# Loading v as bf16 with a casting DMA instead of casting it on VectorE and ScalarE

## The chip, the cores and the metric

One core of one Trainium2 chip. The metric is the device time of one execution in microseconds (us); lower is better. The profile's span is about 1.7 us shorter than that time, because it leaves out what lies before the first and after the last instruction. In the profile's lines PE is TensorE (matrix products), DVE is VectorE, ACT ScalarE, POOL GpSimd and SP SyncE; L332 is line 332 of that run's kernel, so one statement has different numbers in different runs.

## The reference

A recurrence over time for each of 16 sequences and 256 channels: a weighted mean of v with running exponential weights built from k, w and u, kept stable by a running maximum. Cut to its core:

```python
# k, v: (16, 2048, 256) float32; w, u: (256,)
for b in range(batch):
    aa = bb = 0; pp = -1e38                       # 256 channels each; shortened
    for t in range(seq_len):
        kk, vv = k[b, t, :], v[b, t, :]
        ww = u + kk
        qq = np.maximum(pp, ww)
        e1 = np.exp(pp - qq)
        e2 = np.exp(ww - qq)
        output[b, t, :] = (e1 * aa + e2 * vv) / (e1 * bb + e2 + 1e-08)
        ww = pp - w + kk
        qq = np.maximum(ww, kk)
        e1 = np.exp(ww - qq)
        e2 = np.exp(kk - qq)
        aa = e1 * aa + e2 * vv
        bb = e1 * bb + e2
        pp = qq
```

## The kernel before

It replaces the recurrence by matrices. Time is cut into chunks of 126 steps, four sequences are one "pair" of tiles (126 x 1024 numbers of k, as many of v; four pairs are one "step" below), and there are 66 pairs (64, and 2 of a short first chunk, the "head"). For each pair: VectorE rounds k (L281), PE multiplies it to exponents X, ScalarE takes one long exponential of X (L313), VectorE multiplies by v (L332), PE forms the sums for the state, the denominator and the numerator, ScalarE inverts the denominator by a logarithm (L517) and an exponential (L522), VectorE multiplies numerator and inverse, and a DMA stores the result. A pair's output follows ten pairs later. The parts that the argument touches, condensed ("..." marks cuts; slices and names are shortened):

```python
AHEAD = 4; HALVES = 8
SHARED = range(2, HALVES)               # pairs whose v ScalarE casts
kpool = tile_pool(bufs=AHEAD); vpool = tile_pool(bufs=AHEAD); vbpool = tile_pool(bufs=2)

def load(n):                            # four pairs ahead
    kr = kpool.tile([128, 4, Dm], F32); vr = vpool.tile([128, 4, Dm], F32)
    ...
        for t, x in ((kr, k), (vr, v)): # k first, then v; SyncE for n < 2, else GpSimd
            K((SP if n < 2 else POOL).dma_start(out=t[0:r, :, :], in_=x[...]))

def round_k(n):
    ...
    K(DVE.tensor_copy(KM[n][0:r, 0:i, :], kr_of.pop(n)[0:r, 0:i, :]))

def cast_v(n):
    vb = vbpool.tile([128, 4, Dm], BF16, tag="vb", name="vb")
    if n in SHARED:
        K(SC.activation(vb[0:r, 0:i, :], vr_of.pop(n)[0:r, 0:i, :], ACT.Copy))
    else:
        K(DVE.tensor_copy(vb[0:r, 0:i, :], vr_of.pop(n)[0:r, 0:i, :]))

def times_v(n):
    K(DVE.tensor_mul(ez[0:r, 1:4:2], ez[0:r, 0:4:2], vb...))

def log_den(n): K(SC.activation(RD[n], DEN[n], ACT.Ln, scale=RS))
def invert(n):  K(SC.activation(RD[n], RD[n], ACT.Exp, scale=-1.0))

matrices_for_sums(); round_k(0); logs(0); cast_v(0)
for n in range(NP + LAG + 2):           # the order on each engine, cut
    load(n + AHEAD); exps(n); round_k(n + 1); num(qp, 0); invert(qi)
    den(q); log_den(q); mult(qp, 0); cast_v(n + 1); logs(n + 1)
    num(qp, 1); times_v(n); sums(n); mult(qp, 1); store(qp)
```

`K` pins each engine's instructions to this order, so an engine that waits for one operand lets nothing later pass.

Of the kernel before, what the change touches and what calls it, by code (L numbers as in the profile page):

```python
# [7 lines left out]
F32 = mybir.dt.float32  # L8
F32R = mybir.dt.float32r
BF16 = mybir.dt.bfloat16  # L10
ALU = mybir.AluOpType
ACT = mybir.ActivationFunctionType
# [10 lines left out]
def kernel(  # L23
# [11 lines left out]
    def K(ins):  # L35

        block, e, new = nc.cur_bb.bb, ins.ins.engine, []
        for i in reversed(block.instructions):
            if i.engine == e:
                new.append(i)  # L40
                if i.name == pinned.get(e):
                    break
        for a, b in zip(new[1:], new):
            tc.add_manual_dep(b, a.name, mybir.DependencyInfo(
                mybir.DependencyClass.NoSync, mybir.DependencyReason.DATA), reason="order")
        pinned[e] = new[0].name
        return ins

    PE, DVE, SC, POOL, SP = nc.tensor, nc.vector, nc.scalar, nc.gpsimd, nc.sync

    B, T, Dm = k.shape
    HS = 63
    TC = 2 * HS
    T0 = T % TC
    NST = T // TC
    D = 2 * Dm
    GB = T0
    NG = 3
    NH = NG * GB
    AHEAD = 4  # L60
    LAG = 10
    HALVES = 8

    SHARED = range(2, HALVES)
    RS = 2.0 ** -43
    LNRS = 43 * 0.6931471805599453
    CAP = 68.0
# [2 lines left out]
    consts = ctx.enter_context(tc.tile_pool(name="consts", bufs=1))  # L70
    kpool = ctx.enter_context(tc.tile_pool(name="kpool", bufs=AHEAD))
    vpool = ctx.enter_context(tc.tile_pool(name="vpool", bufs=AHEAD))
    vbpool = ctx.enter_context(tc.tile_pool(name="vbpool", bufs=2))
    ezpool = ctx.enter_context(tc.tile_pool(name="ezpool", bufs=7))
    rpool = ctx.enter_context(tc.tile_pool(name="rpool", bufs=5))
    small = ctx.enter_context(tc.tile_pool(name="small", bufs=2))
# [13 lines left out]
    pairs = []  # L90
# [6 lines left out]
    kr_of, vr_of = {}, {}  # L97

    def is_head(n):
        return pairs[n][0] < 0  # L100
# [5 lines left out]
    def tiles_of(n):  # L106
        return 1 if pairs[n] == (-1, 1) else 2
# [5 lines left out]

    def load(n):
        kr = kpool.tile([128, 4, Dm], F32, tag="kr", name="kr")
        vr = vpool.tile([128, 4, Dm], F32, tag="vr", name="vr")
        kr_of[n], vr_of[n] = kr, vr
        c, p = pairs[n]
        if is_head(n):
            if p == 1:  # L120
                K(POOL.memset(kr[64:96, 0:2, :], 0.0))
                K(POOL.memset(vr[64:96, 0:2, :], 0.0))
            for t, x in ((kr, k), (vr, v)):
                for g in range(NG):
                    b = 6 * g + 4 * p
                    e = min(b + 2 * tiles_of(n), B)
                    if b < e:
                        K(SP.dma_start(out=t[g * GB:(g + 1) * GB, 0:e - b, :],
                                        in_=x[b:e, 0:T0, :].rearrange("n t d -> t n d")))
        else:  # L130
            t0 = T0 + c * TC
            r = min(128, T - t0)
            for t, x in ((kr, k), (vr, v)):
                K((SP if n < 2 else POOL).dma_start(  # L134
                    out=t[0:r, :, :], in_=x[4 * p:4 * p + 4, t0:t0 + r, :].rearrange("n t d -> t n d")))


    crow = consts.tile([128, Dm], F32, tag="crow", name="crow")
# [7 lines left out]
    for n in range(2):  # L146
        load(n)
# [8 lines left out]
    def select(ap, cmp, fill, base, cm, n, step):  # L156
        K(POOL.affine_select(out=ap, in_=ap, pattern=[[step, n]], compare_op=cmp,
                             fill=fill, base=base, channel_multiplier=cm))
# [21 lines left out]
    K(POOL.memset(cc[:, 5:6], CAP - LNRS))  # L180
    select(cc[:, 4:5], GE, 0.0, -HS, 1, 1, 0)
    select(cc[:, 4:5], GE, 0.0, TC - 1, -1, 1, 0)

    def head_blocks(f):
        fill(f[0:GB, GB:NH], 0.0)
        fill(f[GB:2 * GB, 2 * GB:NH], 0.0)
# [87 lines left out]
    def round_k(n):  # L274
        r = NH if is_head(n) else TC
        i = 2 * tiles_of(n)
        if is_head(n):
            KM[n] = kmh.pop(0)
        else:
            KM[n] = kms[n % 2]  # L280
        K(DVE.tensor_copy(KM[n][0:r, 0:i, :], kr_of.pop(n)[0:r, 0:i, :]))  # L281

    def logs(n):
        kr = NH + 2 if is_head(n) else 128


        if n == HALVES:
            psx[0] = log_banks("psx")
        if n < HALVES:
            X = [psx[0].tile([128, 2, D], F32, tag=f"X{q}", name=f"X{q}") for q in range(2)]  # L290
        else:
            t = psx[0].tile([128, 2, 2, D], F32, tag="X", name="X")
            X = [t[:, 0], t[:, 1], t]
        km = KM.pop(n).rearrange("p (i n) d -> p i (n d)", i=2)
        for q, m in enumerate((NLEh, NLZh) if is_head(n) else (NLE, NLZ)):
            for i in range(tiles_of(n)):
                K(PE.matmul(X[q][:, i, :], m[0:kr, :], km[0:kr, i, :], start=True, stop=True))  # L297
        X_of[n] = X

    def ez_of(n):  # L300
        j = 2 * (n % 2)
        return EZ[n // 2][:, :, j:j + tiles_of(n), :]

    def exps(n):
        if n % 2 == 0:
            EZ[n // 2] = ezpool.tile([128, 4, 4, D], BF16, tag="ez", name="ez")
        i = tiles_of(n)
        X = X_of.pop(n)
        if n < HALVES:
            for q in range(2):  # L310
                K(SC.activation(ez_of(n)[:, 2 * q], X[q][:, 0:i, :], ACT.Exp))  # L311
        else:
            K(SC.activation(ez_of(n)[:, 0:4:2], X[2][:, :, 0:i, :], ACT.Exp))  # L313

    VB = {}

    def cast_v(n):
        r = NH if is_head(n) else TC
        i = 2 * tiles_of(n)
        vb = vbpool.tile([128, 4, Dm], BF16, tag="vb", name="vb")  # L320
        if n in SHARED:
            K(SC.activation(vb[0:r, 0:i, :], vr_of.pop(n)[0:r, 0:i, :], ACT.Copy))  # L322
        else:
            K(DVE.tensor_copy(vb[0:r, 0:i, :], vr_of.pop(n)[0:r, 0:i, :]))  # L324
        VB[n] = vb

    def times_v(n):
        ez = ez_of(n)
        i = tiles_of(n)
        r = NH if is_head(n) else TC  # L330
        vb = VB.pop(n).rearrange("p (i n) d -> p i (n d)", i=2)
        K(DVE.tensor_mul(ez[0:r, 1:4:2], ez[0:r, 0:4:2],  # L332
                         vb[0:r, 0:i, :].unsqueeze(1).broadcast_to([r, 2, i, D])))



# [156 lines left out]
    def widen():  # L493
        first_phase.close()
        for name, bufs in (("den", 1), ("num", 2)):
            wide.append(ctx.enter_context(tc.tile_pool(name="wide" + name, bufs=bufs, space=bass.MemoryType.PSUM)))
# [22 lines left out]
    def invert(n, a=0, b=None):  # L519
        r = rows_of(n)  # L520
        b = tiles_of(n) if b is None else b
        K(SC.activation(RD[n][0:r, a:b, :], RD[n][0:r, a:b, :], ACT.Exp, scale=-1.0))  # L522
# [47 lines left out]
    def small_work(n, where):  # L570
        for f, args in later.pop((n, where), []):
            f(*args)
# [38 lines left out]
    matrices_for_sums()  # L611
    round_k(0)
    logs(0)
    cast_v(0)

    out_at = {n + (LAG - 4 if is_head(n) else LAG): n for n in range(NP)}
    for n in range(NP + LAG + 2):

        q, qi, qp = out_at.get(n), out_at.get(n - 1), out_at.get(n - 2)
        live, more, out_q, out_qi, out_qp = n < NP, n + 1 < NP, q is not None, qi is not None, qp is not None  # L620
        if n == NP:
            widen()
        if n + AHEAD < NP:
            load(n + AHEAD)
        small_work(n, "a3")
        if live:
            exps(n)
        small_work(n, "d0")
        if more:
            round_k(n + 1)  # L630
        small_work(n, "p0")
        if out_qp:
            num(qp, 0)
            if n > NP:
                num(qp, 1)
        small_work(n, "d1")
        small_work(n, "a0")
        small_work(n, "p1")
        if n == NP:
            num(qp, 1)  # L640
        if out_qi and qi < NP - 1:
            invert(qi)
        small_work(n, "a2")
        if out_q:
            if q not in DEN:
                den(q)
            if n == NP + 1:

                den(q + 1)
            if q < NP - 1:  # L650
                log_den(q)
            else:
                for i in range(2):
                    log_den(q, i, i + 1)
                    invert(q, i, i + 1)
        if out_qp:
            mult(qp, 0)
        small_work(n, "d2")
        if more:
            cast_v(n + 1)  # L660
        small_work(n, "d3")
        small_work(n, "a4")
        if more:
            logs(n + 1)
        if live and out_qp:
            num(qp, 1)
        small_work(n, "p3")
        if live:
            times_v(n)
            sums(n)  # L670
        small_work(n, "p2")
        small_work(n, "d4")
        if out_qp:
            mult(qp, 1)
            store(qp)
        small_work(n, "d5")
        small_work(n, "p4")
        small_work(n, "a1")
# [31 lines left out]
```

## Time and profile before

| | before |
|---|---|
| time, median of 3 runs | 321.77 us (321.7 to 326.54) |
| span of the profiled run | 318.9 us |
| start, to the first long exponential L313 | 36.77 us |
| next seven pairs, to the L313 at 63.68 us | 26.91 us |
| regular stage, 50 pairs, to 282.45 us | 218.77 us |
| tail | 36.45 us |

The prediction shows the busy totals, the steps of the regular stage and its groups. In the groups of the same seven regular steps (count, then busy us and mean ns, then idle time before and what ended it), the long exponential, and the rounding of k:

```profile
L313 ACT ACTIVATE ez<-X 128x2048 bf16<-128x2048 f32 x28 | 52.4, 1873 | 3.6 <-PE num L530 3.3
...
L281 DVE CAST km<-kr 126x1024 fp32r<-126x1024 f32 x28 | 19.0, 680 | 0.0
```

The rounding took 680 ns, against 777 for v's cast of the same size. Of v's casts the 14 that overlapped with one DMA issue of GpSimd took 685 ns and the 14 that overlapped with two took 868. And VectorE's timeline in the first 20 us (start, duration, instruction, and in brackets the idle time before it with its releaser):

```profile
7.29 0.69 DVE L324 CAST vb<-vr 126x1024 bf16<-126x1024 f32 x1 [0.49 <-DMA vr<-in_v_dram]
8.87 0.70 DVE L281 CAST km<-kr 126x1024 fp32r<-126x1024 f32 x1 [0.88 <-DMA kr<-in_k_dram]
...
17.82 0.42 DVE L281 CAST kmh<-kr 96x512 fp32r<-96x512 f32 x1 [2.46 <-DMA kr<-in_k_dram]
```

The second rounding of k stands at 8.87 us behind the first cast of v, and at 17.82 us VectorE has stood 2.46 us for a load of k that was queued behind loads of v.

### The profile page before, as it was taken

What the parts mean: (1) busy time and instruction counts of PE and PEld (TensorE: products, weight loads), DVE (VectorE), ACT (ScalarE), POOL (GpSimd) and SP (SyncE); (2) the same over time, 40 slices, a digit from 0 to 9 for tenths busy, and PEclk for the clock granted to TensorE, in tenths of its full rate; (3) what the DMA queues carried; (4) which work ended last, traced back from release to release, by engine and by line L of the source; (5) the groups of instructions that cost most, each with busy time, mean ns of one, the idle gap of its engine ahead of it and who ended that gap; (6) DMA issues with size and microseconds to landing.
All of it is one profiled execution on the core that took longest, in us unless ns stands there. A gap on an engine that the chain in (4) does not pass through costs nothing. (4 is left out here: it accounts for less than half of the span.)

```text
span 318.9 us, 3968 instructions
## 1 busy us (share of the span) xinstructions
PE 277.0 (87%) x1132; PEld 125.3 (39%) x1132; DVE 277.7 (87%) x561; ACT 277.6 (87%) x318; POOL 167.3 (52%) x224
## 2 busy tenths in 40 slices
PE   1787699799999999999999999999999999888960
PEld 1323344344434444444444444444444444333420
DVE  5758879989999999999999999999999999887760
ACT  6679699599898989999898989899998989698990
POOL 7445428656465665465665646565546665112430
PEclk9999999999999999999999999999999999999995
DMA  6999996999999999999999999999999999944885
GB/s 203 277 332 348 349 328 159 337 329 344 353 351 352 347 365 377 375 341 350 375 380 367 366 366 373 363 346 373 373 369 351 347 322 306 290 170 163 286 257 154
DMA packets 34486, 102.97 MB, mean 323 GB/s; under 512 B 6618, under 2 KB 10478, under 8 KB 34464
## 3 DMA queue, kind: packets, MB, share of 16 engines
q0 software_dynamic: 27248, 98.23, 89.8%
q1 hardware_dynamic: 7184, 4.47, 5.4%
q8 instruction: 9, 0.15, 0.2%
q14 instruction: 13, 0.11, 0.1%
q10 hardware_dynamic: 32, 0.02, 0.0%
HBM read 68.12 MB, written 34.05 MB: 320 GB/s over the span
## 5 line engine op out<-in xcount | busy, mean ns | idle before, releaser
L313 ACT ACTIVATE ez<-X 128x2048 bf16<-128x2048 f32 x58 | 108.6, 1873 | 7.6 <-PE num L530 5.2
L558 POOL DMA_DIRECT2D out_dram<-rd x63 | 53.4, 847 | 117.6 <-issue 40.9
L538 DVE TENSOR_TENSOR rd<-num,rd 128x512 f32<-128x512 f32 (+2 forms) x131 | 88.7, 685 | 11.1 <-ACT rd L522 6.2
L332 DVE TENSOR_TENSOR ez<-ez,vb 126x2048 bf16<-126x2048 bf16 (+1 forms) x66 | 79.7, 1207 | 3.7 <-ACT ez L311 3.1
L517 ACT ACTIVATE rd<-den 128x1024 f32<-128x1024 f32 (+3 forms) x67 | 66.9, 998 | 12.2 <-PE den L508 11.6
L522 ACT ACTIVATE rd<-rd 128x1024 f32<-128x1024 f32 (+3 forms) x67 | 69.3, 1035 | 0.3
L297 PE MATMUL X<-km,NLE 128*128 128x512 f32 x128 | 51.8, 486 | 13.9 <-DVE km L281 9.9
L134 POOL DMA_DIRECT2D kr<-in_k_dram x62 | 56.4, 910 | 11.1 <-DVE km L281 3.6
L134 POOL DMA_DIRECT2D vr<-in_v_dram x62 | 49.9, 806 | 7.8 <-ACT vb L322 4.8
L530 PE MATMUL num<-ez,LfN 128*128 128x512 bf16 x128 | 49.2, 384 | 4.1 <-DVE rd L538 0.8
L530 PE MATMUL num<-ez,IdN 126*128 126x512 bf16 (+1 forms) x131 | 49.8, 380 | 0.0
L324 DVE CAST vb<-vr 126x1024 bf16<-126x1024 f32 x60 | 45.6, 760 | 1.2 <-DMA vr<-in_v_dram 1.1
L362 PE MATMUL tot<-ez,OHV 126*48 126x512 bf16 x128 | 38.9, 385 | 7.7 <-DVE ez L332 6.6
L281 DVE CAST km<-kr 126x1024 fp32r<-126x1024 f32 x64 | 44.0, 687 | 1.9 <-DMA kr<-in_k_dram 1.9
L297 PE MATMUL X<-km,NLZ 128*128 128x512 f32 x128 | 40.9, 402 | 0.1
L362 PE MATMUL tot<-ez,OHE 128*48 128x512 bf16 x128 | 40.1, 395 | 0.0
L508 PE MATMUL den<-ez,Id 126*128 126x512 bf16 (+1 forms) x131 | 39.1, 378 | 0.0
L508 PE MATMUL den<-ez,Lf 128*128 128x512 bf16 x128 | 38.0, 377 | 0.8 <-DVE tsum L385 0.4
L297 PEld LDWEIGHTS X<-km,NLE 128*128 128x128 f32 x128 | 23.6, 192 | 26.7 <-DVE km L281 6.9
L297 PEld LDWEIGHTS X<-km,NLZ 128*128 128x128 f32 x128 | 24.4, 192 | 6.5 <-ACT ez L311 1.0
L362 PEld LDWEIGHTS <-OHV 126*48 126x48 bf16 x128 | 13.4, 104 | 29.5 <-issue 20.4
L530 PEld LDWEIGHTS <-LfN 128*128 128x128 bf16 x128 | 12.3, 96 | 28.6 <-issue 25.5
(104 smaller groups left out, 204.6 us busy)
## 6 DMA issues: line engine op xcount, KB each, us to landing
out_dram<-rd POOLq DMA_DIRECT2D x60, 512.0 KB, 7.0
kr<-in_k_dram POOLq DMA_DIRECT2D x58, 512.0 KB, 7.9
vr<-in_v_dram POOLq DMA_DIRECT2D x58, 512.0 KB, 8.5
kr<-in_k_dram POOLq DMA_DIRECT2D x4, 504.0 KB, 10.7
vr<-in_v_dram POOLq DMA_DIRECT2D x4, 504.0 KB, 12.0
kr<-in_k_dram SPq DMA_DIRECT2D x2, 512.0 KB, 5.0
vr<-in_v_dram SPq DMA_DIRECT2D x2, 512.0 KB, 6.1
ez<-row SPq DMA_DIRECT2D x64, 8.0 KB, 6.3
```

What stands on the lines that cost most here:

```text
L134: K((SP if n < 2 else POOL).dma_start(out=t[0:r, :, :], in_=x[4 * p:4 * p + 4, t0:t0 + r, :].rearrange("n t d -> t n d")))
L297: K(PE.matmul(X[q][:, i, :], m[0:kr, :], km[0:kr, i, :], start=True, stop=True))
L313: K(SC.activation(ez_of(n)[:, 0:4:2], X[2][:, :, 0:i, :], ACT.Exp))
L324: K(DVE.tensor_copy(vb[0:r, 0:i, :], vr_of.pop(n)[0:r, 0:i, :]))
L332: K(DVE.tensor_mul(ez[0:r, 1:4:2], ez[0:r, 0:4:2], vb[0:r, 0:i, :].unsqueeze(1).broadcast_to([r, 2, i, D])))
L362: K(PE.matmul(TOT[c], m[0:r, :], ez_of(n)[0:r, q, i, :], start=n == first_of[c] and i == 0 and q == 0, stop=n == last_of[c] and i == tiles ...
L508: K(PE.matmul(d[:, i, :], m[0:r, :], ez_of(n)[0:r, q, i, :], start=q == 0, stop=q == 2, skip_group_check=True))
L517: K(SC.activation(RD[n][0:r, a:b, :], DEN[n][0:r, a:b, :], ACT.Ln, scale=RS))
L522: K(SC.activation(RD[n][0:r, a:b, :], RD[n][0:r, a:b, :], ACT.Exp, scale=-1.0))
L530: K(PE.matmul(d, m[0:r, :], ez_of(n)[0:r, q, i, :], start=q == 1, stop=q == 3, skip_group_check=True))
L538: K(DVE.tensor_mul(RD[n][0:r, i, :], NUM.pop((n, i))[0:r, :], RD[n][0:r, i, :]))
L558: K(eng.dma_start(out=out[4 * p + a:4 * p + b, t0:t0 + r, :].rearrange("n t d -> t n d"), in_=o[0:r, a:b, :]))
```

## The change

v is to arrive as bf16: the DMA casts it, only GpSimd's queue issues it, and no engine casts it. So the 60 casts on VectorE, the 6 on ScalarE and their buffers go; the multiplication reads the loaded tile. The first two loads of v follow GpSimd's setup, so that the start of k is not delayed.

```diff
-        vr = vpool.tile([128, 4, Dm], F32, tag="vr", name="vr")
+        vr = vpool.tile([128, 4, Dm], BF16, tag="vr", name="vr")
 ...                                        # head: k on SyncE, v on GpSimd
-            for t, x in ((kr, k), (vr, v)):
-                K((SP if n < 2 else POOL).dma_start(
-                    out=t[0:r, :, :], in_=x[4 * p:4 * p + 4, t0:t0 + r, :]...))
+            K((SP if n < 2 else POOL).dma_start(
+                out=kr[0:r, :, :], in_=k[4 * p:4 * p + 4, t0:t0 + r, :]...))
+            if n >= 2:
+                load_v(n)                   # POOL.dma_start into vr_of[n]
 ...                                        # after GpSimd's setup of masks:
+    for n in range(2):
+        load_v(n)
 ...
-    def cast_v(n): ...                      # and vbpool, SHARED, both calls
 ...
-        vb = VB.pop(n).rearrange("p (i n) d -> p i (n d)", i=2)
+        vb = vr_of.pop(n)[:, 0:2 * i, :].rearrange("p (i n) d -> p i (n d)", n=2)
```

More of the change, by code (lines that the diff above doesn't have):

```diff
@@ L62 @@
     HALVES = 8
-    SHARED = range(2, HALVES)
     RS = 2.0 ** -43
@@ L72 @@
     vpool = ctx.enter_context(tc.tile_pool(name="vpool", bufs=AHEAD))
-    vbpool = ctx.enter_context(tc.tile_pool(name="vbpool", bufs=2))
     ezpool = ctx.enter_context(tc.tile_pool(name="ezpool", bufs=7))
@@ L122, in load @@
                 K(POOL.memset(vr[64:96, 0:2, :], 0.0))
-            for t, x in ((kr, k), (vr, v)):
+            for t, x, eng in ((kr, k, SP), (vr, v, POOL)):
                 for g in range(NG):
@@ L127, in load @@
                     if b < e:
-                        K(SP.dma_start(out=t[g * GB:(g + 1) * GB, 0:e - b, :],
+                        K(eng.dma_start(out=t[g * GB:(g + 1) * GB, 0:e - b, :],
                                         in_=x[b:e, 0:T0, :].rearrange("n t d -> t n d")))
@@ L132, in load, with load_v @@
             r = min(128, T - t0)
-            for t, x in ((kr, k), (vr, v)):
-                K((SP if n < 2 else POOL).dma_start(
-                    out=t[0:r, :, :], in_=x[4 * p:4 * p + 4, t0:t0 + r, :].rearrange("n t d -> t n d")))
+            K((SP if n < 2 else POOL).dma_start(
+                out=kr[0:r, :, :], in_=k[4 * p:4 * p + 4, t0:t0 + r, :].rearrange("n t d -> t n d")))
+            if n >= 2:
+                load_v(n)
+    def load_v(n):
+        c, p = pairs[n]
+        t0 = T0 + c * TC
+        r = min(128, T - t0)
+        K(POOL.dma_start(out=vr_of[n][0:r, :, :],
+                         in_=v[4 * p:4 * p + 4, t0:t0 + r, :].rearrange("n t d -> t n d")))
     crow = consts.tile([128, Dm], F32, tag="crow", name="crow")
@@ L313, in exps @@
             K(SC.activation(ez_of(n)[:, 0:4:2], X[2][:, :, 0:i, :], ACT.Exp))
-    VB = {}
-    def cast_v(n):
-        r = NH if is_head(n) else TC
-        i = 2 * tiles_of(n)
-        vb = vbpool.tile([128, 4, Dm], BF16, tag="vb", name="vb")
-        if n in SHARED:
-            K(SC.activation(vb[0:r, 0:i, :], vr_of.pop(n)[0:r, 0:i, :], ACT.Copy))
-        else:
-            K(DVE.tensor_copy(vb[0:r, 0:i, :], vr_of.pop(n)[0:r, 0:i, :]))
-        VB[n] = vb
     def times_v(n):
@@ L330, in times_v @@
         r = NH if is_head(n) else TC
-        vb = VB.pop(n).rearrange("p (i n) d -> p i (n d)", i=2)
+        vb = vr_of.pop(n)[:, 0:2 * i, :].rearrange("p (i n) d -> p i (n d)", n=2)
         K(DVE.tensor_mul(ez[0:r, 1:4:2], ez[0:r, 0:4:2],
-                         vb[0:r, 0:i, :].unsqueeze(1).broadcast_to([r, 2, i, D])))
+                         vb[0:r].unsqueeze(1).broadcast_to([r, 2, i, D])))
     TOT, SUMS = {}, {}
@@ L613 @@
     logs(0)
-    cast_v(0)
     out_at = {n + (LAG - 4 if is_head(n) else LAG): n for n in range(NP)}
@@ L658 @@
         small_work(n, "d2")
-        if more:
-            cast_v(n + 1)
         small_work(n, "d3")
```

## The prediction

> **What bounds the kernel now.** I read the page first: busy shares, then the 40 slices.
>
> ```profile
> PE 277.0 (87%) x1132; PEld 125.3 (39%) x1132; DVE 277.7 (87%) x561; ACT 277.6 (87%) x318; POOL 167.3 (52%) x224
> ...
> DVE  5758879989999999999999999999999999887760
> ...
> DMA  6999996999999999999999999999999999944885
> GB/s 203 277 332 348 349 328 159 337 329 344 353 351 352 347 365 377 375 341 350 375 380 367 366 366 373 363 346 373 373 369 351 347 322 306 290 170 163 286 257 154
> ```
>
> Three engines have equal totals, so totals decide nothing. The slices show a start (to about 60 us), a long even middle, and a tail from about 285 us. In the tail nothing is multiplied by v any more (the last casts of v start at 280.3 us), so the change can only act in the first two.
>
> In the timeline of ScalarE the long exponential (L313) repeats with a pattern of four: 119.66, 137.11, 154.46 and so on. One such step is four pairs of tiles. The stretches view over these steps, cut at those starts, gives two neighbouring steps and the mean of seven (us busy by engine, then clock, DMA share, GB/s):
>
> ```profile
> 154.46:171.89 17.43, 16.48 (x70) 7.52 (x70) 16.73 (x33) 16.14 (x19) 10.00 (x13) 1.00 1.03 377
> 171.89:189.22 17.33, 16.39 (x70) 7.53 (x70) 16.63 (x33) 16.15 (x19) 10.35 (x13) 1.00 1.02 365
> ...
> sum 121.81, PE 115.03 PEld 52.70 DVE 116.95 ACT 113.01 POOL 71.47; mean PE 16.43 PEld 7.53 DVE 16.71 ACT 16.14 POOL 10.21
> ```
>
> A step lasts 121.81 / 7 = 17.40 us. VectorE fills 16.71 of it (96%), PE 16.43 (its ends are modelled, so that is too much), ScalarE 16.14. VectorE is the bound, by little. The groups of the same seven steps say what it does and why the other two wait (count, busy us, mean ns, then idle before and its releaser):
>
> ```profile
> L332 DVE TENSOR_TENSOR ez<-ez,vb 126x2048 bf16<-126x2048 bf16 x29 | 35.2, 1213 | 0.0
> L517 ACT ACTIVATE rd<-den 128x1024 f32<-128x1024 f32 x28 | 28.5, 1018 | 5.2 <-PE den L508 5.2
> L134 POOL DMA_DIRECT2D vr<-in_v_dram x28 | 22.3, 795 | 0.0
> L324 DVE CAST vb<-vr 126x1024 bf16<-126x1024 f32 x28 | 21.8, 777 | 0.0
> L362 PE MATMUL tot<-ez,OHV 126*48 126x512 bf16 x56 | 16.6, 377 | 3.0 <-DVE ez L332 2.4
> L475 PE MATMUL den<-It,ab 128*128 128x128 bf16 x7 | 1.6, 229 | 2.0 <-DVE ab L469 2.0
> ```
>
> ScalarE idles 5.2 us at L517 and 3.6 us at L313, 8.8 in 7 steps: 1.26 us of each step, all of its gap (17.40 - 16.14), always released by PE. PE in turn idles 3.0 + 2.0 us for VectorE's results. So ScalarE's gap is VectorE's lateness passed on through PE.
>
> **What the Trainium skill says.** (1) "VectorE: DVE Perf Modes", section "Mode 2×_2P": a single-source fp32 copy with both ends in SBUF yields two results per cycle; with that page's 0.96 GHz and some 150 cycles of overhead, (1024 / 2 + 150) / 0.96 = 690 ns. The trace agrees: the casts of v have a median of 687 ns. (2) "SBUF — State Buffer", section "Who interferes with whom": such a cast takes the port pair shared with GpSimd for the whole instruction, and GpSimd's descriptor writing and the cast block each other. The trace agrees in kind: the casts range from 679 to 997 ns and GpSimd's issues from 748 to 1306. Removing the casts removes both. (3) "DMA: Bandwidth & Descriptors", section "SWDGE vs HWDGE vs iDMA": a cast in a DMA must be issued by GpSimd. That fits the change, which moves v's first loads off SyncE; this trace has no casting DMA. (4) The same page, section "Where 436 GB/s comes from": the 16 engines share a ceiling of 435 GB/s. The trace reaches 366 over these steps, 377 in its best step and 380 in its best slice. No page that I found gives the rate of a casting DMA; that is the large unknown here.
>
> **The change part by part.** The order of instructions on each engine was compared: VectorE 540 to 480 rows (60 casts gone), ScalarE 320 to 314 (6 casts gone), PE unchanged at 1755, GpSimd 209 to 213, SyncE 14 to 9. No other compute instruction moves relative to its neighbours.
>
> VectorE in the middle: four casts a step, 21.8 / 7 = 3.1 us. It falls from 16.7 to 13.6 us a step. The multiplication L332 reads bf16 in the same shape as before, so it should stay at 1213 ns. VectorE then stops being the bound, and what is left is ScalarE at 16.14 us a step, untouched there (its six casts of v are all before 32.2 us).
>
> ScalarE's limit: of its 1.26 us idle per step I leave 0.3, since the dependence of L517 on PE remains. Step 16.45 us, 0.95 saved. The regular stage runs from the L313 at 63.68 to the one at 282.45: 51 pairs, 12.75 steps. 12.75 x 0.95 = 12.1 us.
>
> DMA's limit: a step moves 366 GB/s x 17.40 us = 6.37 MB (1.57 MB for each pair's k, v and output, and small rows). If a casting load costs what a plain one does, the best step's 377 GB/s gives 16.9 us and the best slice's 380 gives 16.8. Then only 0.5 to 0.6 us a step can be had: some 7 us.
>
> Start: ScalarE spends 5.9 us on six casts (mean 989 ns) between 14 and 32 us, where it is 85% busy (17.08 of 20 us in the stretch 20 to 40). I count half, 3 us, and give 1 back because v's first seven transfers now follow GpSimd's setup and go through one queue. Net 2 us.
>
> GpSimd: 10.21 us of 17.40 busy. Its v issue would have to grow from 0.80 to over 2.6 us (7.2 us of slack over four) before it binds. Hidden.
>
> Buffers: v's slot is now released by L332 rather than by the cast, nearly a pair later. It is needed again by the L332 four pairs on, 17 us, and v lands in 8.6 us (at most 9.6 between 100 and 200 us). Hidden too.
>
> Sum: 321.8 - 12.1 - 2 = 307.7 if ScalarE sets the pace, 321.8 - 7 - 2 = 312.8 if the DMA engines do. I take 310.
>
> **The rivals.**
>
> *The DMA engines become the bound at plain cost.* For it:
>
> ```profile
> out_dram<-rd POOLq DMA_DIRECT2D x60, 512.0 KB, 7.0
> kr<-in_k_dram POOLq DMA_DIRECT2D x58, 512.0 KB, 7.9
> vr<-in_v_dram POOLq DMA_DIRECT2D x58, 512.0 KB, 8.5
> ```
>
> These are DMA issues with their size and the median us to landing. A pair's three transfers at 377 GB/s need 4.2 us together, but each takes 7 to 8.5: the queue is already deep. Against it: VectorE waits for a load only 1 us in all for v and 1.9 + 2.5 for k. The output tiles are recycled after five pairs; a store issued at the end of the third and landing 7 us later leaves L517 about 2.5 us of slack, so this is where saturation would show first. Result 312 to 316.
>
> *The casting DMA is slower than a plain one*, per byte or because its bf16 runs are half as long (now 98.23 MB in 27,248 packets, 3.6 KB each). Then DMA sets the step outright: at 1.5 times the cost for v a step is 6.37 x 3.5 / 3 / 0.377 = 19.7 us, the whole about 349; at twice, 22.5 us and 385. Nothing in the profile speaks against it. That the writer kept the other two transfers plain and placed v's loads with care is weak evidence that it pays.
>
> *The casting DMA is cheaper*, since it writes half the bytes: a step could then move in 6.37 x 2.5 / 3 / 0.377 = 14.1 us. ScalarE binds, giving 305 to 309.
>
> *PE is the next bound instead of ScalarE.* In the tail, matmuls of 512 columns start 0.22 us apart; 64 of them a step are 14.1 us, and I estimate 15 with the small ones. Below ScalarE, so at most it keeps 0.5 us more of the idle time: 313 or so.
>
> **Range and chances.** I give cheaper or equal casting 75% (305 to 316, nearly all of it more than 2% faster, that is under 315.3), slower casting 20% (over 328), and 5% to a loss elsewhere that cancels the gain. Range 302 to 336: the floor is ScalarE with no gaps at all in the middle (1.26 x 12.75 = 16 us) and 4 us at the start; the top takes in a casting load some 20% dearer. Faster 0.66, within 2% 0.15, slower 0.19.
>
> **What would show it right or wrong.** Right: VectorE's total near 277.7 - 45.6 = 232 us, ScalarE's near 272, the pattern of L313 at 16.3 to 16.9 us a step with ScalarE over 96% busy, and PE's waits for VectorE nearly gone. DMA as bound: new idle time at L517 released by the output's DMA, or at the casts of k and at the multiplication released by a load, with landing times over 9 us. Wrong: v's landing at 12 us or more, a step longer than 17.4 us, GB/s lower at an unchanged DMA share, or many more packets of under 2 KB.

## The result, and the profile after

Before's runs are the three of above and a fourth.

| | runs | median | lowest to highest |
|---|---|---|---|
| before | 4 | 323.56 us | 321.70 to 326.54 |
| after | 4 | 300.01 us | 299.37 to 302.48 |

The ratio is 0.9306, 95% interval 0.9223 to 0.9389. Here and below a ratio is the mean time of one kernel's fast runs over that of the other's in the same rounds, so it is not quite the ratio of the medians quoted. The outcome, with a correct result, is faster by 6.9%; it lies below the forecast range of 302 to 336.

The page of after (busy totals, VectorE's slices, the granted TensorE clock in 40 slices of 7.5 us, and the queue that carries k, v and the output: packets, MB, share):

```profile
PE 271.8 (90%) x1132; PEld 124.5 (41%) x1132; DVE 248.3 (83%) x501; ACT 270.3 (90%) x312; POOL 160.7 (53%) x231
...
DVE  4777768967998989999998999898989898878660
...
PEclk9995999999999999999999999999999999999996
...
q0 software_dynamic: 52896, 82.78, 101.6%
```

VectorE fell below PE and ScalarE. The packets nearly doubled (27,248 to 52,896); the share is the time that packets took, and it passes 100% where they overlap. The "5" in the clock row, at 23 to 30 us, makes this profiled run the slowest of the four (302.48 us): its start is disturbed. The start of e3 below, which only adds copies that turn out harmless and had no such dip, serves as the undisturbed one:

| stage | before | after (this run) | e3 (no dip) |
|---|---|---|---|
| to the first long exponential | 36.77 | 35.06 | 32.90 |
| next seven pairs | 26.91 | 25.39 | 25.50 |
| regular stage, 50 pairs | 218.77 | 203.80 | 202.52 |
| tail | 36.45 | 36.55 | 35.58 |
| span | 318.9 | 300.8 | 296.5 |

In the stretches view each row of after is eight pairs, so two of the steps of before (length, then us busy by engine, clock, DMA share, GB/s):

```profile
146.18:178.34 32.16, 32.02 (x139) 14.93 (x139) 29.51 (x57) 31.80 (x37) 18.71 (x24) 1.00 1.17 330
178.34:210.48 32.14, 32.02 (x139) 14.90 (x139) 29.50 (x57) 31.79 (x36) 18.72 (x24) 1.00 1.17 329
...
sum 128.57, PE 128.04 PEld 59.55 DVE 118.04 ACT 127.19 POOL 75.16; mean PE 32.01 PEld 14.89 DVE 29.51 ACT 31.80 POOL 18.79
```

A step is 128.57 / 8 = 16.07 us, where it was 17.40. ScalarE fills 31.80 of 32.14 (98.9%), PE 32.01 by its modelled ends, VectorE 29.51 (92%). The groups of these four rows:

```profile
L322 ACT ACTIVATE ez<-X 128x2048 bf16<-128x2048 f32 x33 | 62.0, 1879 | 1.7 <-PE num L527 1.5
...
L329 DVE TENSOR_TENSOR ez<-ez,vr 126x2048 bf16<-126x2048 bf16 x33 | 40.2, 1217 | 0.0
...
L514 ACT ACTIVATE rd<-den 128x1024 f32<-128x1024 f32 x32 | 32.7, 1021 | 0.0
...
L290 DVE CAST km<-kr 126x1024 fp32r<-126x1024 f32 x32 | 26.5, 828 | 0.0
...
L359 PE MATMUL tot<-ez,OHV 126*48 126x512 bf16 x64 | 19.1, 379 | 0.0
...
L472 PE MATMUL den<-It,ab 128*128 128x128 bf16 x8 | 1.8, 229 | 0.1
```

L514 is L517 of before: its idle time, 5.2 us in seven steps, is gone altogether; 1.7 us in eight steps remain at the long exponential (L313, now L322; 3.6 in seven before). PE's waits for VectorE, 3.0 and 2.0 us before, are down to 0.0 and 0.1 (L359, L472). The multiplication by v is as fast as before (1217 against 1213 ns). The rounding of k (L281, now L290) grew from 680 to 828 ns. The DMA issues of after (size, median us to landing):

```profile
out_dram<-rd POOLq DMA_DIRECT2D x60, 512.0 KB, 7.5
kr<-in_k_dram POOLq DMA_DIRECT2D x58, 512.0 KB, 8.1
vr<-in_v_dram POOLq DMA_DIRECT2D x60, 256.0 KB, 7.2
```

v lands sooner than before (7.2 against 8.5 us), k and the output a little later (8.1 against 7.9, 7.5 against 7.0).

### The profile page after: what moved, and what is told of

The parts are those of the page before. It is cut to its first block, busy times and chain, and to the rows that moved or that the text cites. A ratio compares the mean times of both kernels' runs of the same rounds, so it can differ in the third digit from the quotient of the medians.

```text
span 300.8 us, 3949 instructions
## 1 busy us (share of the span) xinstructions
PE 271.8 (90%) x1132; PEld 124.5 (41%) x1132; DVE 248.3 (83%) x501; ACT 270.3 (90%) x312; POOL 160.7 (53%) x231
## 2 busy tenths in 40 slices
DMA packets 58485, 85.94 MB, mean 286 GB/s; under 512 B 6834, under 2 KB 42406, under 8 KB 58464
## 3 DMA queue, kind: packets, MB, share of 16 engines
q0 software_dynamic: 52896, 82.78, 101.6%
HBM read 68.12 MB, written 34.05 MB: 340 GB/s over the span
## 5 line engine op out<-in xcount | busy, mean ns | idle before, releaser
L322 ACT ACTIVATE ez<-X 128x2048 bf16<-128x2048 f32 x58 | 108.9, 1877 | 3.3 <-PE num L527 1.8
L329 DVE TENSOR_TENSOR ez<-ez,vr 126x2048 bf16<-126x2048 bf16 (+1 forms) x66 | 79.8, 1209 | 4.1 <-ACT ez L320 2.0
L555 POOL DMA_DIRECT2D out_dram<-rd x63 | 52.6, 835 | 48.0 <-issue 17.9
L514 ACT ACTIVATE rd<-den 128x1024 f32<-128x1024 f32 (+3 forms) x67 | 67.0, 1000 | 4.4 <-PE den L505 3.4
L290 DVE CAST km<-kr 126x1024 fp32r<-126x1024 f32 x64 | 51.2, 801 | 3.0 <-DMA kr<-in_k_dram 3.0
L130 POOL DMA_DIRECT2D kr<-in_k_dram x62 | 47.4, 764 | 0.2 <-issue 0.2
L359 PE MATMUL tot<-ez,OHE 128*48 128x512 bf16 x128 | 40.5, 399 | 0.0
L359 PE MATMUL tot<-ez,OHV 126*48 126x512 bf16 x128 | 39.1, 387 | 1.0 <-DVE ez L329 0.9
L359 PEld LDWEIGHTS <-OHV 126*48 126x48 bf16 x128 | 13.6, 106 | 17.6 <-issue 4.9
L505 PEld LDWEIGHTS <-Lf 128*128 128x128 bf16 x128 | 12.4, 98 | 19.9 <-issue 6.6
```

The source lines that it names most:

```text
L322: K(SC.activation(ez_of(n)[:, 0:4:2], X[2][:, :, 0:i, :], ACT.Exp))
L329: K(DVE.tensor_mul(ez[0:r, 1:4:2], ez[0:r, 0:4:2], vb[0:r].unsqueeze(1).broadcast_to([r, 2, i, D])))
L359: K(PE.matmul(TOT[c], m[0:r, :], ez_of(n)[0:r, q, i, :], start=n == first_of[c] and i == 0 and q == 0, stop=n == last_of[c] and i == tiles ...
L505: K(PE.matmul(d[:, i, :], m[0:r, :], ez_of(n)[0:r, q, i, :], start=q == 0, stop=q == 2, skip_group_check=True))
L514: K(SC.activation(RD[n][0:r, a:b, :], DEN[n][0:r, a:b, :], ACT.Ln, scale=RS))
L555: K(eng.dma_start(out=out[4 * p + a:4 * p + b, t0:t0 + r, :].rearrange("n t d -> t n d"), in_=o[0:r, a:b, :]))
```

## The experiments

The theory: VectorE's casts were the bound, and taking them away is the whole gain. The rivals: the lighter DMA traffic is the gain or the new limit; the load order or ScalarE's six casts are. Results are medians with lowest and highest; each set ran on one chip, beside runs of the kernel before (medians 320.95 to 323.51 us over the sets). One run each of e1 and e3, and three of before's (327.03 to 328.83 us), counted as slow and are not in the ratios. e6 and e7 have two runs each and their verdict is "unclear"; what is read from them is the step.

**e1, v stays a plain f32 load and nothing casts it.** Its output is wrong, which doesn't matter for the time. The multiplication reads a constant; a one-column copy keeps the wait for v.

```diff
-        vr = vpool.tile([128, 4, Dm], BF16, ...)
+        vr = vpool.tile([128, 4, Dm], F32, ...)
-        vb = vr_of.pop(n)[:, 0:2 * i, :].rearrange(...)
+        K(DVE.tensor_copy(touch[0:r, :], vr_of.pop(n)[0:r, 0, 0:1]))
+        vb = ones[:, 0:2 * i, :].rearrange(...)     # constant bf16 tile
```

> The changed kernel, but v is loaded as plain fp32 (512 KB each, same queue and order) and the multiplication reads a constant bf16 tile; a one-column read of v's tile on VectorE, ahead of the multiplication, keeps the wait for the load and frees its slot. Wrong result on purpose (v is replaced by 1). No engine and no DMA casts v. Theory A (all of the gain is the casts' time on VectorE and ScalarE; the DMA's own cost does not matter): about 300 us, a step of 16.1 us as in the changed kernel. Theory B (DMA relief: at plain cost the 16 engines cap the step at the 377 to 380 GB/s taken for the prediction, so the smaller transfer is needed for the last part of the gain): step 16.8 us, 308 to 312 us, with new idle time at the logarithm of the denominators released by the stores, or at the casts of k.

Measured: 299.97 us (297.34 to 303.17), ratio 0.9276 (0.918 to 0.9371). Two neighbouring steps in the stretches view:

```profile
158.79:190.96 32.17, 31.83 (x137) 14.96 (x139) 29.07 (x65) 31.82 (x37) 18.72 (x25) 1.00 1.03 397
```

The same step as after, at 397 GB/s instead of 329. (The count takes a casting load at its bf16 size; read from HBM are 68.12 MB in before, after and e1 alike.) So the lighter traffic is not needed for the gain, and 377 to 380 GB/s, which I had taken for the DMA engines' limit, was only what the kernel before asked for.

**e2, after with spare casts back on VectorE.** They sit where v's casts were and read rounded k, which is already there: only VectorE's time comes back, without a wait for v.

```diff
+    def spare_cast(n):                    # called where cast_v was
+        if n not in range(2, HALVES):
+            vb = vbpool.tile([128, 4, Dm], BF16, tag="vb", name="vb")
+            K(DVE.tensor_copy(vb[0:r, 0:i, :], KM[n][0:r, 0:i, :].bitcast(F32)))
```

> The changed kernel, with spare casts of the same shape (126x1024 fp32 to bf16, from k's rounded tile into a tile that nobody reads) put back on VectorE at the places of the old ones, for all pairs whose v VectorE used to cast (60). v still comes by casting DMA. Correct result. Theory A: the regular stage goes back to about 17.4 us a step, and the whole to about 317 to 319 (the start keeps its gain). Theory B: a good part of the gain stays, step under 16.9 us, under 312 us.

Measured: 323.28 us (322.08 to 323.79), ratio 1.0013 (0.9926 to 1.0101). All of the gain is gone, with v still arriving as bf16. The step is 17.85 us, longer than before's 17.40, and the time is past the 317 to 319 of theory A. The groups of eight regular steps show why:

```profile
L331 DVE CAST vb<-km 126x1024 bf16<-126x1024 f32 x32 | 27.8, 868 | 0.0
L291 DVE CAST km<-kr 126x1024 fp32r<-126x1024 f32 x32 | 26.3, 822 | 0.0
```

Both kinds of cast are now slowed; e8 takes that up.

**e3, after with the six spare casts back on ScalarE.**

```diff
+        if n in range(2, HALVES):
+            K(SC.activation(vb[0:r, 0:i, :], KM[n][0:r, 0:i, :].bitcast(F32), ACT.Copy))
```

> The changed kernel, with only the six early casts put back on ScalarE (spare ones, same shape and places, from k's rounded tile, read by nobody). Correct result. If the gain of 3.2 us in the start is the six casts that ScalarE no longer makes, 302.5 to 303.5 us; if the start is set by loads or by the chain of k's cast and PE, under 301.

Measured: 298.73 us (298.1 to 303.45), ratio 0.9258 (0.9178 to 0.9338), no slower than after. ScalarE's six casts cost nothing at the start; the 3 us that I counted for them had been no gain.

**e4, after with the copy of the sums moved from ScalarE to VectorE** (0.59 us on ScalarE in each step, out of PSUM, where PE's results lie in this program), to see whether ScalarE binds.

```diff
-        K(SC.activation(ts, TOT.pop(c), ACT.Copy))
+        K(DVE.tensor_copy(ts, TOT.pop(c)))
```

> The changed kernel, with the copy of the sums out of PSUM (48x512, 0.59 us, one a step, 17 in all) moved from ScalarE to VectorE, which has 1.3 us of slack a step. Correct result. If ScalarE sets the step now (15.9 of 16.07 us busy): 0.4 to 0.5 us a step less, 293 to 296 us. If PE does (16.0 of 16.07 us by the modelled ends): 299 to 301, and ScalarE's idle time grows by what was taken off.

Measured: 300.29 us (300.04 to 303.3), ratio 0.9334 (0.9253 to 0.9416), step 16.20 us. No gain, and ScalarE is no longer full: 124.58 of 129.62 us (96%), with new idle time in its groups:

```profile
L322 ACT ACTIVATE ez<-X 128x2048 bf16<-128x2048 f32 x32 | 60.4, 1887 | 2.7 <-PE num L527 2.7
...
L514 ACT ACTIVATE rd<-den 128x1024 f32<-128x1024 f32 x32 | 32.9, 1027 | 2.3 <-PE den L505 2.3
```

By the expectation this is the case in which PE sets the step. But the trial was not clean: it puts the copy on VectorE ahead of the multiplication, on which PE waits. So it neither confirms nor refutes ScalarE as the bound.

**m1 to m4, the transfers by themselves.** Their outputs are wrong, which doesn't matter for the times. Only DMAs, one queue, four slots per input: 64 loads of k, 64 of v, 64 stores in m1 and m2; v alone in m3 and m4. Between the two of a pair only v's tile differs:

```diff
-        vr = vpool.tile([128, 4, Dm], F32, ...)     # m1, m3
+        vr = vpool.tile([128, 4, Dm], BF16, ...)    # m2, m4
```

> DMA traffic alone: the 64 loads of k (512 KB), 64 of v (512 KB, plain fp32) and 64 stores (512 KB) in turn from one GpSimd queue with four slots per input, no computing (wrong result on purpose: ones are stored). This is the DMA floor of the kernel before. Theory B: 16.6 to 17.0 us per four pairs (377 to 380 GB/s), so over 265 us; theory A: clearly under 16 us per four pairs, under 255 us.

> The same traffic with v cast to bf16 by the DMA. If a casting load costs what a plain one does: within 2% of the plain traffic. If its cost follows the bytes written (one sixth of all written bytes less): up to 16% less. If casting is slower per byte: longer than the plain traffic, but under 16 us per four pairs, since the changed kernel runs at 16.07.

> Only the 64 plain loads of v, four slots: 33.5 MB at some 350 to 400 GB/s, 85 to 96 us plus the start.

> Only the 64 casting loads of v: the same time if reads set the pace, half of it if writes do, longer if the cast is slow.

Measured: m1 268.1 us (266.87, 269.34), m2 256.55 us (256.42, 256.68); m3 105.45 and m4 102.88 us, one run each. The queue's row in m1:

```profile
q0 software_dynamic: 27648, 100.68, 100.2%
```

and in m2:

```profile
q0 software_dynamic: 52224, 83.90, 114.7%
```

A casting load of v costs about what a plain one does per byte read (span 101.1 against 103.7 us for v alone), and the mixed traffic takes 4.3% less by the medians (4.8% in the spans, 254.7 against 267.6) although the packets nearly double. Four pairs' plain traffic needs 267.6 / 16 = 16.7 us here, as theory B had it. But that is more than the step that e1 reached with the same loads (16.08): this trial, with four slots (buffers) behind one queue, does not measure the engines' ceiling either.

**e5, before with after's load order only.** v stays plain and cast.

```diff
-            for t, x in ((kr, k), (vr, v)):      # head: SyncE for both
+            for t, x, eng in ((kr, k, SP), (vr, v, POOL)):
 ...                                              # load_v split out of load
+    for n in range(2):                           # after GpSimd's setup
+        load_v(n)
```

> The kernel before (all casts on engines, plain loads), with only the order of the first loads taken from the change: v's first seven transfers leave the SyncE queue and are issued by GpSimd at the places where the change issues them. Correct result. If the start's gain (first ScalarE instruction of L313 at 32.6 to 32.9 us in undisturbed runs of the changed kernel and of its variants, against 36.8) is k's transfers no longer queued behind v's: that instruction at 33 to 34 us, and 318 to 319.5 us in all. If it is the removed casts' waits for v's landing: unchanged, 321 to 323.

Measured: 322.41 us (321.65 to 322.97), ratio 1.0011 (0.9938 to 1.0085). The order alone gains nothing: the first long exponential starts at 38.23 us, later than before's 36.77, because VectorE stands 4.52 us at its first cast for a v that now comes later. With this order the start gains only where VectorE no longer waits for v there (after, against e5 and e12).

**e6, e4 together with e7's relief of PE; e7, PE relieved alone.** Their outputs are wrong, which doesn't matter for the times. One of four matmuls of a pair's sums is left out.

```diff
-            for i in range(tiles_of(n)):                      # e6 and e7
+            for i in range(1 if q == 1 else tiles_of(n)):
-                            stop=n == last_of[c] and i == tiles_of(n) - 1 and q == 1,
+                            stop=n == last_of[c] and i == 0 and q == 1,
-        K(SC.activation(ts, TOT.pop(c), ACT.Copy))            # e6 only
+        K(DVE.tensor_copy(ts, TOT.pop(c)))
```

> The changed kernel with PE and ScalarE both relieved: the second of the two matmuls that sum the v half is left out for each pair (0.22 us of PE per pair, 0.87 us a step; wrong result on purpose), and the copy of the sums is on VectorE as in the run before. If PE sets the changed kernel's step of 16.07 us and ScalarE is next: a step of 15.4 to 15.6 us. If the DMA engines do: still 15.9 to 16.1.

> The changed kernel with PE alone relieved in the same way (wrong result on purpose). If PE sets the step and ScalarE is next, at 15.9 us: 15.85 to 15.95 us a step. If ScalarE and PE bind each other only through their waits: 15.7 or less. If the DMA engines bind: 16.0 to 16.1.

Measured: e6 300.57 us (299.95, 301.19), ratio 0.9335 (0.9225 to 0.9444), step 16.21. e7 298.43 us (298.43, 298.44), ratio 0.9268 (0.9163 to 0.9374), step 16.03. Six steps of e7:

```profile
95.06:191.26 96.20, 91.78 (x391) 42.66 (x391) 87.93 (x169) 95.41 (x109) 56.18 (x72) 1.00 1.17 329
```

With PE down to 95% busy the step hardly moves, and ScalarE stays at 99.2%: PE does not bind. (The expectation had a step of 16.0 to 16.1 under "the DMA engines bind", which e1's 397 GB/s rules out; it had no case in which ScalarE alone binds. e6's step fits none of its cases.) That e6 keeps e4's step says that e4's loss was not PE's lack of time. In e6's timeline one pair of the four is shorter and the next longer (4.66 us); I put that down to the chain from the multiplication through the sums, their copy and the one shared PSUM bank to the next logarithm. No run isolates that chain, so this stays an argument.

**e8, e2 with five slots for v.**

```diff
-    vpool = ctx.enter_context(tc.tile_pool(name="vpool", bufs=AHEAD))
+    vpool = ctx.enter_context(tc.tile_pool(name="vpool", bufs=AHEAD + 1))
```

> The changed kernel with the 60 spare casts on VectorE, as before, and five slots for v instead of four, so that v's load no longer waits for the multiplication to free its slot. Correct result. The run with four slots took 17.85 us a step against 17.40 in the kernel before, with the casts of k at 822 ns instead of 680. If this excess is GpSimd writing v's descriptors just when VectorE's casts want the shared ports: the casts fall back to about 700 to 750 ns and the step to 17.4 to 17.5 us, 316 to 318 us in all. If it comes from elsewhere: unchanged, 322 to 324.

Measured: 318.86 us (318.13 to 319.6), ratio 0.9911 (0.9823 to 0.9998), step 17.45 us. The groups:

```profile
L331 DVE CAST vb<-km 126x1024 bf16<-126x1024 f32 x32 | 25.4, 794 | 0.0
L291 DVE CAST km<-kr 126x1024 fp32r<-126x1024 f32 x32 | 21.8, 680 | 0.0
```

k's rounding is back at 680 ns. In after v's slot comes free only with the multiplication, so GpSimd issues v's load later, and it falls on the rounding of k: the 24 of 32 roundings that overlapped with an issue of v took 877 ns, the other 8 took 682. A fifth slot removes that wait and the overlap. With it, VectorE's time in the middle equals before's and so does the step (17.45 against 17.40): the whole gain of the regular stage is VectorE's time. What is left of the gain, 0.9% (its interval barely leaves out 1), lies at the start, whose first long exponential comes at 33.75 us.

**e9, e3 with the real v as source**, so that ScalarE also waits for v, as before.

```diff
+            K(SC.activation(vb[0:r, 0:i, :], vr_of[n][0:r, 0:i, :], ACT.Copy))   # n in 2..7
```

> The changed kernel with the six early casts back on ScalarE as in the earlier run that cost nothing, but now reading v's own tile, so that they wait for v's landing as the old casts did (bf16 to bf16, same shape, nobody reads the result). If the start's gain is the casts' early wait for v: the first ScalarE exponential over four banks moves from 32.9 us to 34.5 or later, and the whole to 300.5 to 303. If not: 298 to 300, as with the spare casts that read k.

Measured: 299.64 us (298.56 to 301.02), ratio 0.9279 (0.9227 to 0.9331), first long exponential at 32.95 us. ScalarE's casts cost nothing at the start, with their wait or without.

**e10, after with half of each inversion left out**: a relief of ScalarE that gives no other engine more to do. Its output is wrong, which doesn't matter for the time.

```diff
-        K(SC.activation(RD[n][0:r, a:b, :], RD[n][0:r, a:b, :], ACT.Exp, scale=-1.0))
+        K(SC.activation(RD[n][0:r, a:a + 1, :], RD[n][0:r, a:a + 1, :], ACT.Exp, scale=-1.0))
```

> The changed kernel with ScalarE alone relieved, and nothing added on VectorE: the exponential that inverts the denominators runs over half of its columns (0.43 us less per pair, 1.7 us a step; wrong result on purpose). If ScalarE's amount of work sets the step of 16.07 us: 15.5 us or less, the rest being PE or a chain of waits, some 290 us in all. If PE or the DMA engines set it: 16.0 to 16.1 us and 299 to 300.

Measured: 296.56 us (295.02, 298.09), ratio 0.9181 (0.9094 to 0.9268). Eight steps:

```profile
94.61:221.45 126.84, 126.78 (x553) 59.12 (x553) 117.69 (x224) 115.60 (x144) 75.09 (x97) 1.00 1.18 333
```

The step falls to 126.84 / 8 = 15.86 us, by 0.21, though ScalarE got 1.45 us a step less to do ((127.19 - 115.60) / 8). That is neither of the two cases expected. PE's share by its modelled ends says little here, as it was at 99.6% in after too. But ScalarE's idle time, 11.2 us in these eight steps, is now all released by PE, and no two neighbouring starts of matmuls lie more than 0.45 us apart (in before about four a step do). So ScalarE binds after, and PE comes next, 1.3% behind.

**e11, after with five slots for v** (the edit of e8 on after).

```diff
-    vpool = ctx.enter_context(tc.tile_pool(name="vpool", bufs=AHEAD))
+    vpool = ctx.enter_context(tc.tile_pool(name="vpool", bufs=AHEAD + 1))
```

> The changed kernel with five slots for v instead of four, otherwise the same. Correct result. The casts of k should go from 828 ns back to about 680 ns in the even middle. If VectorE is off the path that sets the step: no change, 16.0 to 16.1 us a step, 299 to 301 us in all; if its lateness still shows through: 0.1 to 0.3 us a step, 296 to 298.

Measured: 299.15 us (298.38 to 302.44), ratio 0.9289 (0.9211 to 0.9368), step 16.06 us. k's rounding is back at 684 ns in the even middle, and the time does not change: VectorE is off the path, so the collision with GpSimd is harmless in after. No version that I ran is clearly faster than after and correct.

**e12, after with a VectorE copy of v for the first two pairs only.** This gives back the in-order wait for v at the start and nothing else.

```diff
+        if n < 2:
+            K(DVE.tensor_copy(vb[0:r, 0:i, :], vr_of[n][0:r, 0:i, :]))
```

> The changed kernel with only the first two casts of v back on VectorE at their old places, reading v's own tile (spare: bf16 to bf16, read by nobody), so that VectorE, which works in order, waits for v's landing before it casts the second tile of k and before it builds the head's matrices. The run with only the loads' order changed stood 4.5 us at the first of these. If this wait is what costs the start its gain: the first ScalarE exponential over four banks moves from 32.6 to 33.4 us to 35 to 38 us, and the whole to 302 to 304. If not: no change, and the start's gain stays unexplained.

Measured: 302.92 us (302.62 to 303.14), ratio 0.9379 (0.9324 to 0.9434), first long exponential at 37.32 us. VectorE's timeline in e12:

```profile
11.10 0.43 DVE L330 COPY vb<-vr 126x1024 bf16<-126x1024 bf16 x1 [4.53 <-DMA vr<-in_v_dram]
11.44 0.69 DVE L291 CAST km<-kr 126x1024 fp32r<-126x1024 f32 x1
```

and in after:

```profile
7.62 0.69 DVE L290 CAST km<-kr 126x1024 fp32r<-126x1024 f32 x1 [1.10 <-DMA kr<-in_k_dram]
...
14.07 0.42 DVE L290 CAST kmh<-kr 96x512 fp32r<-96x512 f32 x1
```

Two copies of 0.43 us cost some 3 to 4 us (302.92 against 299.15 to 300.01). They do it by the 4.53 us for which VectorE stands, with the second rounding of k behind it (11.44 instead of 7.62 us): from the first long exponential on, e12 is as fast as e3 (263.9 against 263.6 us to the end).

## Why the prediction was wrong

The mechanism held; the sizes did not. VectorE was the bound, its casts were the reason, and ScalarE sets the pace now. But 14 us of gain were summed where about 22 came (6.94% of some 323), and 2.3 of those 14 were then taken off again for a DMA limit at a rate that e1 exceeds. Three terms failed: ScalarE's step of 16.45 us, the limit of the DMA engines, and the 2 us of the start. Between the two undisturbed profiles, before and e3, the spans differ by 22.4 us: 5.3 in the first two stages, 16.3 in the regular one, 0.8 in the tail.

- **VectorE is the bound, its lateness reaches ScalarE through PE: right.** L517's idle time is gone, PE's waits for VectorE are gone, and e2 and e8 give the regular stage's whole gain back with VectorE's time alone.
- **ScalarE's limit, 16.45 us a step and 12.1 us in the regular stage: mis-sized.** The step is 16.07 us; the stage shrank by 15.0 us (after) to 16.3 us (e3). (It has 50 pairs, 12.5 steps, not 51 and 12.75: 12.1 should have been 11.9.) Two terms were off. First, I left 0.3 us of idle time per step; the rows of after leave 32.14 - 31.80 = 0.34 in two steps, 0.17 in one. Second, I took ScalarE's 16.14 us of records as its floor; at full load the same work shows as 15.90. The timeline shows how. In before, with waits between:

```profile
153.08 1.03 ACT L517 ACTIVATE rd<-den 128x1024 f32<-128x1024 f32 x1 [0.74 <-PE den L508]
154.46 1.88 ACT L313 ACTIVATE ez<-X 128x2048 bf16<-128x2048 f32 x1 [0.35 <-PE num L530]
```

In after, without:

```profile
149.22 1.01 ACT L514 ACTIVATE rd<-den 128x1024 f32<-128x1024 f32 x1
150.12 1.88 ACT L322 ACTIVATE ez<-X 128x2048 bf16<-128x2048 f32 x1
151.88 0.26 ACT L448 ACTIVATE y<-AB 128x64 f32<-128x64 f32 x1
```

Back to back, an instruction starts before the record of the one ahead ends: 150.12 is 0.90 us after 149.22, whose record lasts 1.01; 151.88 is 1.76 after 150.12, recorded at 1.88. Each wait that vanishes takes about 0.1 us of recorded busy time with it; ScalarE had three a step in before and has one in after. The engine's floor was lower than its busy time in a gappy trace.

- **The DMA engines' limit of 16.8 to 16.9 us a step: wrong, and this step failed outright.** It read a demand as a capacity. 377 to 380 GB/s was what a kernel bound by VectorE asked for; e1 moves the same bytes at 397 in a step of 16.08 us. So the 2.3 us between 307.7 and 310 were taken off the gain for nothing. The depth of the queue (each landing 7 to 8.5 us) was no sign of saturation either.
- **The start, 2 us: too small, with the wrong cause.** Over the first two stages of the table it gave 3.2 us in the profiled run with its clock dip and 5.3 in e3. ScalarE's casts, from which I took it, are worth nothing there (e3, e9). It takes two things together: k's loads no longer behind v's, and no wait of VectorE for v ahead of k's rounding. The order alone does nothing (e5), and with the new order the wait alone loses 4.4 us again (e12: 37.32 against 32.90). In before that wait was short (0.49 us) and the one for a load of k long (2.46 us); no run has before's order without the casts, so how the gain divides between the two is not shown.
- **VectorE's total near 232 us: 248.3.** The casts' records of 0.69 us and more counted too much, for the same reason as on ScalarE: in before's timeline one starts at 11.80 and the next instruction at 12.41, so 0.61 us (60 such are some 37 us, not 45.6). And k's roundings grew by 7.2 us (44.0 to 51.2), which "removing the casts removes both" missed: the collision with GpSimd's issues moved from v's casts to k's. In the part on buffers I saw v's slot come free later and asked only whether v would be late, not what else its issue would then meet. It cost nothing, because VectorE is off the path (e11).
- **ScalarE's total near 272 us: 270.3. The multiplication unchanged, GpSimd hidden, v in time: right.**
- **The rivals.** Casting slower than plain: no (m3, m4). Casting cheaper: a little (m1, m2), and without effect on the time (e1). PE as next bound: I estimated 15 us a step from its starts in the tail; e10 shows a step of 15.86 with ScalarE waiting for PE, so ScalarE and PE stand within 1.3% and this rival was nearly true. The sign "many more packets of under 2 KB" appeared (10,478 to 42,406) and was no harm; it should not have stood among the signs of a loss.
- **The range.** Its floor of 302 was 16 us in the middle and 4 at the start, taken off one median (321.8 us). The middle's 16 was about what came (15.0 to 16.3); the start brought up to 5.3, and a little came in the tail, for which nothing was allowed. Before's own runs spread over 320.3 to 328.8 us in all the sets; such a spread deserved a floor some us lower. Most of the range's width went to slow casting, which did not happen.

What stays open: why some runs show an early dip of the TensorE clock, and the chain behind e4 and e6.

## What to carry to other kernels

When an engine that binds at 96% is relieved, the next engine's floor is what its work takes back to back, which the start-to-start distances of its densest stretches show, and not its busy time in a trace full of waits. A bandwidth seen in a kernel that something else binds is a demand, not a limit; before a gain is discounted for it, test it with the suspected transfers left as they are. On an engine that works in order, look at every early wait: what stands behind it may be worth more than the instruction that waits.

## What the Trainium skill lacked or had wrong

- "DMA: Bandwidth & Descriptors", section "SWDGE vs HWDGE vs iDMA", says who may issue a casting DMA but gives no rate. Here 64 casting loads of v (f32 to bf16) took a span of 101.1 us against 103.7 plain, one run each, and the mixed traffic 254.7 against 267.6, with about twice the packets. The same page's section "Where 436 GB/s comes from" says that about 358 GB/s of HBM bind for transfers between HBM and SBUF, without the limit that its section "Measured (HBM→SBUF, 128 partitions, SWDGE, issued from GpSimd)" puts on that figure: it is for both cores that share an HBM. With one core running, e1 moved 397 GB/s in its regular steps and m1 up to 396, still below the 435 that the page names as the ports' ceiling.
- "SBUF — State Buffer", section "Who interferes with whom", says that whoever issues first holds the shared ports for the whole instruction and that the other blocks; it has no size for a cast beside a DMA issue. Here a 126x1024 f32 rounding took 877 ns where it overlapped with GpSimd's issue of a 256 KB load (24 of 32 in after) and 684 on the mean where a fifth buffer kept them apart. In before it began 7 times during the issue of a store, and there the later one did not wait: the rounding kept its 683 ns, and the issue took 1146 instead of 758.
- "Perfetto Trace Analysis", section "Optimizing Scalar/DVE Operations", says that part of an instruction's profiled latency overlaps with the next one. The runs agree (a logarithm recorded at 1.01 us, the next start 0.90 us later). What it lacks is the consequence: busy sums overstate an engine's floor where it waits often, here 16.14 us a step against 15.90 for the same work without the waits.
